# The compression's first layer as 128 adjoining columns, with the position embedding summed on GpSimd

## The chip, the cores and the metric

The kernel runs on one core of a Trainium2 chip. The metric is the device time of one execution in microseconds. The engines are named as in the profile: PE is TensorE (PEld its weight loads), DVE is VectorE, ACT is ScalarE, POOL is GpSimd, SP is SyncE, which issues most DMAs. SBUF is the on-chip memory, PSUM the accumulators that PE writes.

## The reference

A decoder trunk of two layers on one sequence of 256 tokens and 2048 features, all in float32. Layer 1 is HGRN2, a gated linear recurrence; layer 2 is native sparse attention with 16 heads in 4 groups. Each layer has one wide input projection, one output projection and a SiLU gate. What the change touches lies in layer 2: the compression of keys and values, and the softmax attention behind it.

```python
def compress_kv(kv, pe, w1, b1, w2):
    """kv (B,S,G,dk) -> compressed (B,G,n_cmp,dk): blocks of CMP_BLOCK with stride CMP_STRIDE, MLP phi."""
    chunks = kv.reshape(B, S // CMP_STRIDE, CMP_STRIDE, G, dk)
    blocks = jnp.concatenate([chunks[:, m:m + n_cmp] for m in range(ratio)], axis=2)
    blocks = blocks + pe[None, None, :, None, :].astype(blocks.dtype)
    flat = blocks.transpose(0, 3, 1, 2, 4).reshape(B, G, n_cmp, CMP_BLOCK * dk)
    return jax.nn.gelu(flat @ w1 + b1) @ w2
```

A block is 32 tokens, the stride is 16, so each block is two adjoining chunks of 16 positions and there are 15 blocks. `w1` has 32 x 128 rows and 128 columns. The embedding `pe` (32 positions of 128 features) adds the same vector `pe . w1` to the hidden layer of each block. This is done once for keys (K set) and once for values (V set).

## The kernel before

Nearly all the work is float32 matmuls at high precision: each operand is cut into a high part (`hi`, a cast to fp32r, by ACT) and a low part (`lo` = raw - hi, by DVE), and a product is three matmuls, hi.hi, hi.lo and lo.hi (`mm3`) or the like. The weights stream through SBUF in pieces of 128 x 1024 numbers, along a list `plan`. For each piece, SP loads it into one of six `raw` buffers (L126, L1095), ACT writes `hi` (L138), DVE writes `lo` (L148), and PE multiplies (L179 and L181 for the input projections, L156 elsewhere). `flush` walks the list in order: ahead of piece i's products it emits the casts up to piece i+3, the subtractions up to i+2 and the loads. There are four `hi` and four `lo` buffers. Each engine takes its instructions in the order in which the program emits them, and waits for semaphores.

Work that belongs to finished chunks (gathers, gates, attention) is written as generators; `advance` steps each of them once before and once after each piece's products, so one more `yield` moves what follows by half a piece.

The compression: `kc_done` collects the projected keys or values (`kz`, feature by token), `compress` splits them into `kh` and `kl`, and `w1_piece` puts four pieces of `w1` per set between the pieces of the next projection (K set: in the value projection's chunk `C_VC`, V set: in `C_KS`). Each piece has four positions of each half of a block. `compress_products` multiplies, for each of the 16 positions, 66 columns of `kh` and `kl` (64 chunks of the four groups, read with a stride of 16, and two columns that hold the embedding of both halves) by 256 columns of `w1` (both halves), three matmuls a position. `phi` then copies the 66 x 256 sums to SBUF, transposes them on PE (L830), adds both halves and the two embedding columns on DVE (L832 to L837), and goes on with GELU and the second layer.

The attention: for each of four groups, `attend` runs logits, softmax, transposes, `evacuate` (it splits the transposed weights into `ph`, `pl` and, for the compressed blocks, the corner tile `pc`) and `values`. `q_split` splits the queries of the next group, and `gated` applies SiLU to the gate `z` (with two loads of activation tables) and multiplies. The output tile of a group is `ot`.

## Time and profile before

| | |
|---|---|
| median of three runs | 986.13 us (985.73 to 987.29) |
| the profiled execution | 986.4 us, of it the span 984.6 us |
| granted TensorE clock | 0.998 |
| PE busy | 968.7 us, 6735 matmuls |
| DVE busy | 658.3 us, 1275 instructions |
| ACT busy | 569.5 us, 1056 instructions |
| POOL busy | 59.9 us, 154 instructions |
| first and last w1 product, K set | 534.3 to 548.5 us |
| transposes of `phi`, K set and V set | at 551.3 and 580.0 us |

A row of single instructions reads: start (us from the span's start), duration in us, engine, line, operation, what it writes and reads, shape, count, and in brackets the idle time of the engine ahead of it and what ended it. A row of a group reads: line, engine, operation, tiles, shape, count, then total busy us and mean ns of one, then the engine's idle time ahead of them and what ended most of it. A row of a stretch reads: from and to, length, then busy time and count of PE, PEld, DVE, ACT and POOL, the granted clock, the share of the DMA engines and GB/s. Matmuls are pipelined: the pace of PE is the distance from start to start, not the duration. Spans on POOL are rough.

### The profile page before, as it was taken

The numbers are of one execution on the slowest core, as the hardware profiler recorded it, in microseconds if no ns is written. First come the engines' busy times: TensorE is split into PE (matmuls) and PEld (weight loads), VectorE is DVE, ScalarE is ACT, GpSimd is POOL, SyncE is SP. The second block draws the span as 40 slices with busy tenths as digits, with TensorE's granted clock in tenths as the row PEclk, the third lists the DMA queues.
The fourth block names the chain that finished last, engine by engine and source line by source line (L and its number), as shares of the span: only waits on it lengthen the run. The fifth ranks groups of instructions, "written<-read, shape, count | busy, mean of one in ns | idle before, by whom it ended". The sixth has DMA issues, their size and how long they took to land.

```text
span 984.6 us, 17622 instructions
## 1 busy us (share of the span) xinstructions
PE 968.7 (98%) x6735; PEld 838.5 (85%) x6735; DVE 658.3 (67%) x1275; ACT 569.5 (58%) x1056; POOL 59.9 (6%) x154
## 2 busy tenths in 40 slices
PE   9999999999999999999999999999999999999996
PEld 8888888888888888888888888998888888888886
DVE  6796478646864786465566666567777778686654
ACT  6754565456545654554455555467677776875542
POOL 3101000100010001000020000000000000000000
PEclk9999999999999999999999999999999999999999
DMA  9655565556555655566777776565555545546662
GB/s 317 201 172 151 172 192 165 157 171 193 156 166 172 186 158 163 176 222 231 234 218 207 223 229 184 157 198 170 150 152 141 158 130 160 160 130 232 204 215 96
DMA packets 141524, 178.98 MB, mean 182 GB/s; under 512 B 6016, under 2 KB 102880, under 8 KB 141312
## 3 DMA queue, kind: packets, MB, share of 16 engines
q1 hardware_dynamic: 139424, 171.86, 56.8%
q0 software_dynamic: 1680, 5.46, 2.0%
q8 instruction: 53, 0.87, 0.4%
q10 hardware_dynamic: 336, 0.54, 0.1%
q14 instruction: 31, 0.25, 0.1%
HBM read 173.62 MB, written 4.22 MB: 181 GB/s over the span
## 4 chain that ended last, share of the span: by engine, by line
PE 80%; ACT 10%; DVE 6%; issue 2%; DMA 1%; SPq 0%; POOLq 0%; ACTq 0%; POOL 0%; DVEq 0%
PE mainps L156 40%; PE mainps L179 21%; PE mainps L181 11%; PE auxps L156 3%; ACT L L970 2%; ACT hi L138 2%; PE auxps L516 2%; DVE lo L148 1%; DVE L L963 1%; ACT ph L1004 1%; ACT L L979 1%; ACT pc L1006 1%; DMA xt<-in_x_dram 1%; DVE pc L1011 1%; ACT L1073 1%
## 5 line engine op out<-in xcount | busy, mean ns | idle before, releaser
L179 PE MATMUL mainps<-xx,hi 128*128 128x512 f32 x1280 | 454.9, 398 | 0.2 <-DVE Kg L313 0.2
L138 ACT CAST hi<-raw 128x1024 fp32r<-128x1024 f32 (+3 forms) x317 | 328.0, 1039 | 206.6 <-PE mainps L156 142.8
L148 DVE TENSOR_TENSOR lo<-raw,hi 128x1024 fp32r<-128x1024 f32 (+3 forms) x317 | 379.2, 1206 | 92.1 <-ACT hi L138 91.3
L181 PE MATMUL mainps<-xx,lo 128*128 128x256 f32 x1280 | 357.6, 279 | 0.1
L179 PEld LDWEIGHTS mainps<-xx,hi 128*128 128x128 f32 x1280 | 240.2, 188 | 54.6 <-DVE Kg L313 0.6
L181 PEld LDWEIGHTS mainps<-xx,lo 128*128 128x128 f32 x1280 | 241.4, 189 | 0.6 <-DVE lo L148 0.4
L156 PE MATMUL mainps<-hi,xx 128*128 128x512 f32 (+1 forms) x704 | 209.4, 375 | 0.0
L156 PEld LDWEIGHTS mainps<-hi,xx 128*128 128x128 f32 x704 | 128.4, 188 | 23.2
L156 PE MATMUL mainps<-lo,xx 128*128 128x512 f32 (+1 forms) x352 | 131.0, 372 | 0.0
L156 PE MATMUL mainps<-hi,yh 128*128 128x512 f32 (+1 forms) x288 | 106.0, 368 | 0.0
L156 PE MATMUL mainps<-hi,yl 128*128 128x512 f32 (+1 forms) x288 | 105.4, 366 | 0.0
L156 PE MATMUL mainps<-lo,yh 128*128 128x512 f32 (+1 forms) x288 | 105.3, 366 | 0.0
L156 PEld LDWEIGHTS mainps<-lo,xx 128*128 128x128 f32 x352 | 66.1, 188 | 10.4
L156 PEld LDWEIGHTS mainps<-hi,yl 128*128 128x128 f32 x288 | 54.3, 189 | 8.8
L156 PEld LDWEIGHTS mainps<-lo,yh 128*128 128x128 f32 x288 | 54.4, 189 | 8.5
L156 PEld LDWEIGHTS mainps<-hi,yh 128*128 128x128 f32 x288 | 54.4, 189 | 8.4
L970 ACT ACTIVATE L<-L,mx 128x128 f32<-128x128 f32 (+1 forms) x96 | 37.6, 393 | 31.0 <-DVE mx L965 31.0
L313 DVE TENSOR_TENSOR zs<-mainps,zs 128x256 f32<-128x256 f32 x48 | 19.0, 421 | 33.7 <-ACT zs L311 33.7
L567 POOL COPY ST<-S 32x128 f32<-32x128 f32 x32 | 21.6, 675 | 229.8 <-DVE S L524 228.8
L524 DVE COPY_PREDICATED S<-masks,auxps 128x128 f32<-128x128 uint32 x48 | 14.6, 303 | 28.8 <-PE auxps L557 15.9
L1008 DVE TENSOR_TENSOR pl<-auxps,ph 128x512 fp32r<-128x512 f32 (+1 forms) x32 | 17.7, 557 | 22.0 <-ACT ph L1004 20.4
L311 ACT COPY zs<-mainps 128x256 f32<-128x256 f32 x48 | 16.5, 373 | 13.5 <-PE mainps L181 13.2
(257 smaller groups left out, 905.2 us busy)
## 6 DMA issues: line engine op xcount, KB each, us to landing
raw<-in_hgrn_w_in_dram SPq DMA_DIRECT2D x127, 512.0 KB, 4.0
raw<-in_nsa_w_in_dram SPq DMA_DIRECT2D x104, 512.0 KB, 3.8
raw<-in_hgrn_w_out_dram SPq DMA_DIRECT2D x32, 512.0 KB, 4.7
raw<-in_nsa_w_out_dram SPq DMA_DIRECT2D x32, 512.0 KB, 4.0
raw<-in_nsa_w_in_dram SPq DMA_DIRECT2D x10, 420.0 KB, 3.9
xt<-in_x_dram SPq DMA_DIRECT2D x8, 256.0 KB, 7.9
raw<-in_x_dram SPq DMA_DIRECT2D x4, 512.0 KB, 4.2
x_dram<-x POOLq DMA_DIRECT2D x4, 512.0 KB, 6.0
```

The source lines that it names most:

```text
L138: nc.scalar.copy(hi[:, :m], raw[:, :m])
L148: nc.vector.tensor_sub(lo[:, :m], raw[:, :m], hi[:, :m].bitcast(F32))
L156: nc.tensor.matmul(dst, a, b, start=first and n == 0, stop=last and n == 2, skip_group_check=True)
L179: nc.tensor.matmul(ps, hv[:, fs], xx[:, k].rearrange("p a t -> p (a t)"), start=k == 0, stop=False, skip_group_check=True)
L181: nc.tensor.matmul(ps[:, S:], lv[:, fs], xh[:, k], start=False, stop=k == KT - 1, skip_group_check=True)
L311: nc.scalar.copy(o, p[:, S:])
L313: nc.vector.tensor_add(o, p[:, :S], o)
L516: nc.tensor.matmul(dst[32 * b:32 * b + 32, j] if cols == 32 else dst[32 * b:32 * b + 32, :, j], k[:, cs], qs, start=True, stop=True, tile_ ...
L524: nc.vector.copy_predicated(S32, masks[:, i, None, :].to_broadcast([P, 4, 32]), bank[:, n])
L567: nc.gpsimd.tensor_copy(ST[rs, :, 0:3:2, rs], S32[rs].rearrange("p (h t) c -> p h t c", h=2))
L970: nc.scalar.activation(dst, dst, AF.Exp, bias=mx[:, i:i + 1], accum_out=sm[:, i:i + 1])
L1008: nc.vector.tensor_sub(pl[:, ks, hh, :], t, ph[:, ks, hh, :].bitcast(F32))
```

## The change

1. `compress` writes one tile `kk` of 16 positions by 128 columns: for each position, 64 columns of high parts and behind them 64 of low parts. `compress_products` needs two matmuls a position, `w1`'s `hi` and `lo` against these 128 columns. The lo.lo product comes with it. The embedding's two columns are gone.
2. The embedding's share is computed on POOL: as soon as DVE has made `lo` of a w1 piece, `embedding` multiplies the raw piece in place by the embedding (a scalar per feature and position), folds 1024 columns in three additions to 128, and adds these to `pew`, a strip of the scratch tile. In `phi` one matmul with `pew` as stationary side and a column of ones sums over the features.
3. `phi` transposes 128 x 128 twice and adds four parts instead of two.
4. `kk` takes the place of `kh` and `kl`; the groups' output tiles share its buffer as one tile of two halves.
5. In the attention, `q_split` and `gated` get one more `yield` ahead, and `evacuate` handles the corner `pc` between the two pieces of `ph` and `pl`.

```diff
-    def add_own(load, fn, done=None):
-        plan.append((dict(load=load, fn=fn, done=done, before=None), None, bool(done)))
+    def add_own(load, fn, done=None, see=None):
+        plan.append((dict(load=load, fn=fn, done=done, before=None, see=see), None, bool(done)))
...
         nc.vector.tensor_sub(lo[:, :m], raw[:, :m], hi[:, :m].bitcast(F32))
         if kts is None:
+            ch["see"](raw)
             parts[i] = hi, lo
             return
...
-        NS["abs"] = scratch[:66, 256:512]
+        NS["abs"] = scratch[:, 256:512]
+        NS["pew"] = scratch[:, 644:772]
...
-    def compress(name, kz, pe0):
-        ns = NS["p2"]
-        kh = ns.tile([P, 66 * 16], F32R, tag="ot", name="kh")
-        kl = ns.tile([P, 66 * 16], F32R, tag="ot", name="kl")
-        pe = pcol[:, 1, pe0:pe0 + 32]
-        srcs = [(slice(512 * j, 512 * j + 512), kz[j].rearrange("p a t -> p (a t)")) for j in range(2)]
-        srcs.append((slice(1024, 1056), pe))
-        yield
-        for cs, src in srcs:
-            nc.scalar.copy(kh[:, cs], src)
-        yield
-        yield
-        for cs, src in srcs:
-            nc.vector.tensor_sub(kl[:, cs], src, kh[:, cs].bitcast(F32))
-        NS[name] = [t.rearrange("p (m q) -> p m q", q=16) for t in (kh, kl)]
+    def compress(name, kz):
+        kk = NS["kk"] = NS["p2"].tile([P, 16, P], F32R, tag="kk", name="kk", bufs=1)
+        by_position = lambda part, j: kk[:, :, 64 * part + 32 * j:64 * part + 32 * j + 32].rearrange("p q m -> p m q")
+        srcs = [(j, flat(kz[j]).rearrange("p (m q) -> p m q", q=16)) for j in range(2)]
+        yield
+        for j, src in srcs:
+            nc.scalar.copy(by_position(0, j), src)
+        yield
+        yield
+        for j, src in srcs:
+            nc.vector.tensor_sub(by_position(1, j), src, by_position(0, j).bitcast(F32))
...
-            kh, kl = NS[name]
-            wh, wl = (t.rearrange("p (a q c) -> p a q c", a=2, q=4) for t in (wh, wl))
+            kk = NS["kk"]
+            parts_ = [t.rearrange("p (a q c) -> p a q c", a=2, q=4) for t in (wh, wl)]
             for q in range(4):
-                mm3(NS[name, "ps"][:66, :256], kh[:, :, 4 * i + q], kl[:, :, 4 * i + q], wh[:, :, q, :], wl[:, :, q, :],
-                    i == 0 and q == 0, i == 3 and q == 3)
+                for n, w in enumerate(parts_):
+                    nc.tensor.matmul(NS[name, "ps"][:, :256], kk[:, 4 * i + q, :], w[:, :, q, :],
+                                     start=i == 0 and q == 0 and n == 0, stop=i == 3 and q == 3 and n == 1,
+                                     skip_group_check=True)
...
+    def embedding(pe0, i):
+        def see(raw):
+            w, acc = raw.rearrange("p (a q c) -> p a q c", a=2, q=4), NS["pew"]
+            pe = pcol[:, 1, pe0 + 4 * i:pe0 + 4 * i + 4]
+            pe = bass.AP(tensor=pe.tensor, offset=pe.offset, ap=[list(pe.ap[0]), [16, 2], [1, 4], [0, P]])
+            nc.gpsimd.tensor_tensor(w, w, pe, op=ALU.mult)
+            for n in (512, 256, 128):
+                nc.gpsimd.tensor_tensor(raw[:, :n], raw[:, :n], raw[:, n:2 * n], op=ALU.add)
+            if i == 0:
+                nc.gpsimd.tensor_copy(acc, raw[:, :P])
+            else:
+                nc.gpsimd.tensor_tensor(acc, acc, raw[:, :P], op=ALU.add)
+        return see
...
-            nc.tensor.transpose(abt[:, a * 66:(a + 1) * 66], abs_[:, a * P:(a + 1) * P], ident[:66, :66])
+            nc.tensor.transpose(abt[:, a * P:(a + 1) * P], abs_[:, a * P:(a + 1) * P], ident)
+        nc.tensor.matmul(abt[:, 256:257], NS["pew"], NS["one"], start=True, stop=True)
         yield
-        nc.vector.tensor_add(bia, b1, abt[:, 64:65])
-        nc.vector.tensor_add(bia, bia, abt[:, 66 + 65:66 + 66])
-        av = abt[:, 0:64].rearrange("p (g m) -> p g m", g=G)
-        bv = abt[:, 66:130].rearrange("p (g m) -> p g m", g=G)
+        nc.vector.tensor_add(bia, b1, abt[:, 256:257])
+        av, al, bv, bl = (abt[:, 64 * n:64 * n + 64].rearrange("p (g m) -> p g m", g=G) for n in range(4))
         nc.vector.tensor_scalar(hid, av[:, :, :NCMP], bia, None, op0=ALU.add)
+        nc.vector.tensor_add(hid, hid, al[:, :, :NCMP])
         nc.vector.tensor_add(hid, hid, bv[:, :, 1:])
+        nc.vector.tensor_add(hid, hid, bl[:, :, 1:])
...
     def q_split(g, a, q):
+
+        yield
...
-            for t, ks in srcs:
+
+            for n, (t, ks) in enumerate(srcs):
                 nc.scalar.copy(ph[:, ks, hh, :], t)
-            for tt in range(2):
-                nc.scalar.copy(pc[64:64 + NCMP, tt], t2[32 * tt:32 * tt + NCMP, 256:384])
-            for t, ks in srcs:
+                for tt in range(2 - 2 * n):
+                    nc.scalar.copy(pc[64:64 + NCMP, tt], t2[32 * tt:32 * tt + NCMP, 256:384])
+            for n, (t, ks) in enumerate(srcs):
                 nc.vector.tensor_sub(pl[:, ks, hh, :], t, ph[:, ks, hh, :].bitcast(F32))
...
-                    ot = ns.tile([P, 66 * 16], F32, tag="ot", name="ot")
...
+                    if g == 0:
+                        NS["ot"] = ns.tile([P, 2, 1024], F32, tag="kk", name="ot", bufs=1)
+                    ot = NS["ot"][:, g % 2]
...
     def gated(g, zs):
         ks = [slice(4 * g + 2 * a, 4 * g + 2 * a + 2) for a in range(2)]
+        yield
         for a in range(2):
             nc.scalar.activation(zs[a], zs[a], AF.Silu)
...
-        return lambda: add_own(load, compress_products(name, i), done if i == 3 else None)
+        return lambda: add_own(load, compress_products(name, i), done if i == 3 else None, embedding(pe0, i))
```

Three places of the order show what moves. First, POOL between the opening of layer 2 and the attention. Before (`Vc` and `pc` are cleared, `scratch` gets the second layer's weights, `bias` is the attention's bias):

```order
L771 MEMSET scratch 128x4
L775 MEMSET Vc 128x512
L775 MEMSET pc 128x512
L776 DMA scratch<-in_nsa_phi_k_w_dram 128x128
L777 DMA scratch<-in_nsa_phi_v_w_dram 128x128
L928 DMA bias<-bias_dram 128x2x256 x2
```

Now, up to the second w1 piece of the K set:

```order
L779 DMA scratch<-in_nsa_phi_v_w_dram 128x128
L829 TENSOR_TENSOR raw<-raw,pcol 128x1024
L831 TENSOR_TENSOR raw<-raw 128x512
L831 TENSOR_TENSOR raw<-raw 128x256
L831 TENSOR_TENSOR raw<-raw 128x128
L833 COPY scratch<-raw 128x128
L829 TENSOR_TENSOR raw<-raw,pcol 128x1024
```

Five operations for each of eight w1 pieces now stand between the weights' loads and the bias loads; `scratch` in them is the strip `pew`, and from the second piece of a set on the copy is an addition at L835.

Second, PE at the end of a set, where the transposes of `phi` lie in the stream of the next projection. Before:

```order
L179 MATMUL mainps<-xx,hi 128x512
L181 MATMUL mainps<-xx,lo 128x256
L830 MATMUL auxps<-ident,scratch 128x66 x2
L179 MATMUL mainps<-xx,hi 128x512
L181 MATMUL mainps<-xx,lo 128x256
```

Now:

```order
L180 MATMUL mainps<-xx,hi 128x512
L182 MATMUL mainps<-xx,lo 128x256
L846 MATMUL auxps<-ident,scratch 128x128 x2
L847 MATMUL auxps<-one,scratch 128x1
L180 MATMUL mainps<-xx,hi 128x512
L182 MATMUL mainps<-xx,lo 128x256
```

The matmul with `pew` (L847) is new, and stands at the same place as the transposes, ahead of the next piece's products.

Third, ACT where a gate's SiLU and an evacuation meet in the attention. Before:

```order
L311 COPY zs<-mainps 128x256 x2
L1073 ACT_TABLE_LOAD
L1073 ACTIVATE zs<-zs 128x512 x2
L1076 ACT_TABLE_LOAD
L1076 ACTIVATE one<-one 128x1
L138 CAST hi<-raw 128x1024
L1004 CAST ph<-auxps 128x4x128
L1004 CAST ph<-auxps 128x2x128
L1006 CAST pc<-auxps 15x128 x2
L138 CAST hi<-raw 128x1024
L1085 CAST yh<-zs 128x512
```

Now:

```order
L312 COPY zs<-mainps 128x256 x2
L138 CAST hi<-raw 128x1024
L1024 CAST ph<-auxps 128x4x128
L1026 CAST pc<-auxps 15x128 x2
L1024 CAST ph<-auxps 128x2x128
L1097 ACT_TABLE_LOAD
L1097 ACTIVATE zs<-zs 128x512 x2
L1100 ACT_TABLE_LOAD
L1100 ACTIVATE one<-one 128x1
L138 CAST hi<-raw 128x1024 x2
```

The SiLU with its two table loads went from ahead of the evacuation to behind it, and `pc` went between the two pieces of `ph`.

More of the change, by code (lines that the diff above doesn't have):

```diff
@@ L784, in zs_take, with kc_done @@
         return z
-    def kc_done(name, *args):
+    def kc_done(name):
         def done(a, ps):
@@ L825, in phi @@
         hid, t1 = hid_all[:, :, :NCMP], NS["gelu"][:, :, :NCMP]
-        nc.scalar.copy(abs_, ab[:66, :256])
+        nc.scalar.copy(abs_, ab[:, :256])
         yield
@@ L1002, in evacuate @@
             pc = NS["pc"][:, hh]
-            for t, ks in srcs:
+            for n, (t, ks) in enumerate(srcs):
                 nc.scalar.copy(ph[:, ks, hh, :], t)
-            for tt in range(2):
-                nc.scalar.copy(pc[64:64 + NCMP, tt], t2[32 * tt:32 * tt + NCMP, 256:384])
-            for t, ks in srcs:
+                for tt in range(2 - 2 * n):
+                    nc.scalar.copy(pc[64:64 + NCMP, tt], t2[32 * tt:32 * tt + NCMP, 256:384])
+            for n, (t, ks) in enumerate(srcs):
                 nc.vector.tensor_sub(pl[:, ks, hh, :], t, ph[:, ks, hh, :].bitcast(F32))
-            nc.vector.tensor_copy(pc[0:NCMP], pc[64:64 + NCMP].bitcast(F32))
-            for tt in range(2):
-                nc.vector.tensor_sub(pc[32:32 + NCMP, tt], t2[32 * tt:32 * tt + NCMP, 256:384],
-                                     pc[64:64 + NCMP, tt].bitcast(F32))
+                if n == 0:
+                    nc.vector.tensor_copy(pc[0:NCMP], pc[64:64 + NCMP].bitcast(F32))
+                for tt in range(2 - 2 * n):
+                    nc.vector.tensor_sub(pc[32:32 + NCMP, tt], t2[32 * tt:32 * tt + NCMP, 256:384],
+                                         pc[64:64 + NCMP, tt].bitcast(F32))
         def values(a, half):
@@ L1087, in gated, with w1_piece @@
             nc.vector.tensor_sub(yl[:, ks[a]], zs[a], yh[:, ks[a]].bitcast(F32))
-    def w1_piece(name, w1, i, b1, finish):
+    def w1_piece(name, w1, i, b1, pe0, finish):
         wv = w1[0].rearrange("(a q d) c -> d a q c", a=2, d=P)
```

14 lines of the change are left out of this document (7 added, 7 removed).

## The prediction

> **What bounds the kernel now.** I read the page first (engine shares), then the chain of waits over the compression's stretch, then the groups of TensorE instructions with the idle time ahead of them in the attention, and last single instructions on GpSimd and VectorE.
>
> ```profile
> span 984.6 us, 17622 instructions
> ...
> PE 968.7 (98%) x6735; PEld 838.5 (85%) x6735; DVE 658.3 (67%) x1275; ACT 569.5 (58%) x1056; POOL 59.9 (6%) x154
> ```
>
> TensorE (PE) is busy for 98% of the span. VectorE (DVE) is at 67%, GpSimd (POOL) at 6%. The busy time by stage, and the chain between 525 and 600 us, where the compression lies:
>
> ```profile
> 530.00:560.00 30.00, 30.00 (x190) 26.90 (x188) 20.58 (x30) 16.75 (x22) 0.00 (x0) 1.00 0.71 212
> ...
> 700.00:890.00 190.00, 184.10 (x1132) 163.02 (x1131) 144.87 (x404) 139.93 (x342) 5.51 (x18) 1.00 0.52 153
> ```
>
> ```profile
> by line: PE mainps L179 55.4%; PE mainps L181 27.8%; PE auxps L156 15.4%; PE auxps L875 1.3%; PE auxps L830 0.3%; PE auxps L869 0.2%
> ```
>
> In the compression PE never waits (30.00 of 30.00), so each matmul less is time less, and each wait that is put ahead of PE is time more. In the attention PE idles 5.9 of 190 us. POOL does nothing from 530 to 560 us.
>
> **The matmuls that go.** One w1 piece of the compression, its first and last row, and the rows ahead of it and behind it:
>
> ```profile
> 534.20 0.28 PE L181 MATMUL mainps<-xx,lo 128*128 128x256 f32 x1
> 534.32 0.28 PE L156 MATMUL auxps<-hi,kh 128*66 128x256 f32 x1
> ...
> 535.62 0.28 PE L156 MATMUL auxps<-hi,kl 128*66 128x256 f32 x1
> 535.74 0.40 PE L179 MATMUL mainps<-xx,hi 128*128 128x512 f32 x1
> ```
>
> Twelve matmuls take 535.74 - 534.32 = 1.42 us, 0.119 us each. Four of twelve go in each of 8 pieces: 32 x 0.119 = 3.8 us. The stationary side grows from 66 to 128 columns; the row ahead has 128 and streams 256 columns too, and the next matmul starts 0.12 us after it (534.20 to 534.32), so I add nothing for that. In each `phi`, the two transposes grow from 66 to 128 columns and one matmul by a single column is added; before, the two took 0.10 us (551.28 to 551.38 below). I put 0.2 us each, 0.4 together. Sum: -3.4 us.
>
> **The attention's order.** The groups with idle time ahead of them, 700 to 895 us:
>
> ```profile
> L156 PE MATMUL auxps<-Kh,qh 128*128 128x272 f32 (+1 forms) x36 | 10.6, 294 | 1.2 <-DVE pl L1008 1.2
> L156 PE MATMUL auxps<-ph,Vsh 128*128 128x256 f32 x19 | 5.8, 303 | 3.0 <-DVE pc L1011 2.7 <-ACT ph L1004 0.2
> L156 PE MATMUL auxps<-pl,Vsh 128*128 128x256 f32 x19 | 5.7, 298 | 0.9 <-DVE pl L1008 0.9
> L1029 PE MATMUL auxps<-pc,Vc 79*128 79x256 f32 x13 | 4.0, 305 | 1.4 <-ACT hi L138 1.4
> ```
>
> ScalarE (ACT) around the first slow place:
>
> ```profile
> 734.51 1.28 ACT L1073 ACT_TABLE_LOAD   x1
> ...
> 738.26 0.20 ACT L1076 ACTIVATE one<-one 128x1 f32<-128x1 f32 x1
> 739.31 0.85 ACT L1004 CAST ph<-auxps 128x512 fp32r<-128x512 f32 x2
> ```
>
> 1.2 + 3.0 + 0.9 + 1.4 = 6.5 us. Ahead of the evacuation at 739.31 stands the SiLU with its two table loads, from 734.51 to 738.46, about 4 us; the added `yield` in `gated` puts it behind. That frees the 2.7 and the 1.2. The corner `pc` now comes ahead of the second piece of `pl`, which serves the 1.4; `q_split`'s `yield` takes a copy away from ahead of the evacuation, which serves the 0.9. Behind the moved SiLU wait the next `hi` casts and `exps`; before, they stood behind SiLU and evacuation both, so they lose nothing. Bounds 0 (as much comes back elsewhere) and 6.5; I take 5.2, four fifths, since SiLU's 3.9 is the plain part: -5.2 us.
>
> **GpSimd's sum, and the new wait.** Per w1 piece POOL now makes five operations: 1024, 512, 256, 128 and 128 columns, 2048 in all, serially dependent. The last sum of a set is the stationary side of a matmul in `phi`. PE takes its instructions in order, so the whole weight stream behind that matmul waits for POOL. That wait is not in the trace; its ends are.
>
> ```profile
> masks.py:199 POOL TENSOR_SCALAR_AFFINE_SELECT ident<-ident 128x128 f32<-128x128 f32 x1 | 0.3, 291 | 0.1
> ...
> L78 POOL TENSOR_SCALAR rs<-oss 128x4 f32<-128x4 f32 x8 | 1.5, 192 | 113.8 <-ACT y L617 113.8
> ```
>
> ```profile
> 114.73 0.19 POOL L78 TENSOR_SCALAR rs<-oss 128x4 f32<-128x4 f32 x1 [25.62 <-ACT y L617]
> 115.00 1.05 POOL L79 TENSOR_TENSOR rs<-rs,mhalf 128x4 f32<-128x4 f32 x1
> ```
>
> *Price.* With one input, (291 - 192) / 124 = 0.80 ns a column. Fixed are 0.19 us for four columns, and 115.00 - 114.73 = 0.27 until the next, dependent operation starts. A two-input operation has three streams: 0.8 ns a column if all overlap, 1.6 if the reads take turns, 2.4 to 2.5 if all do. I take 2.0, between the last two: POOL and VectorE take turns at their operands (the next rows), so I don't expect two reads of POOL's own to overlap. A piece: 2048 x 2.0 = 4.10 + 5 x 0.27 = 5.45 us unopposed; the ends are 2.99 and 6.47.
>
> The Trainium skill (GPSIMD Engine Reference, Performance versus the Vector engine) gives 4497 ns for a two-input add over 2048 columns, so (4497 - 192) / 2048 = 2.1 ns each as an estimate; by it, the sum below would be about 1.2 us higher. No run here shows it.
>
> *Contention.* POOL's copies in the first layer beside VectorE:
>
> ```profile
> L567 POOL COPY ST<-S x32: 292/392/1271, 69.5 to 385.3; 32x128 f32<-32x128 f32 x32
> ```
>
> ```profile
> 85.57 1.22 DVE L148 TENSOR_TENSOR lo<-raw,hi 128x1024 fp32r<-128x1024 f32 x1
> 85.73 1.21 POOL L567 COPY ST<-S 32x128 f32<-32x128 f32 x1 [13.95 <-DVE S L524]
> 86.71 0.51 DVE L501 TENSOR_TENSOR QL<-QL,TT 128x256 f32<-128x256 f32 x1
> ```
>
> ```profile
> L501 DVE TENSOR_TENSOR QL<-QL,TT x32: 414/420/514, 54.5 to 389.5; 128x256 f32<-128x256 f32 x32
> ```
>
> The copy that takes 0.29 us at best started at 85.73, inside a `lo` subtraction, and ended at 86.94, 0.15 after it; the next DVE operation, with two inputs from SBUF too, took 0.51 instead of 0.42, as long as the copy's 128 columns last. So they take turns whole, and `lo` is such an operation.
>
> The Trainium skill (SBUF — State Buffer, SBUF: two separate sides) says so: GpSimd and a VectorE operation with two SBUF inputs take one port pair as an exclusive lock for the whole instruction. The rows above agree. If they shared instead, the tally's figure without turns would be nearer.
>
> *The tally.* The second w1 piece of the K set is the first of the three `lo` at 535.99, done by 537.2. The row, VectorE's `lo` from there to `phi`, and PE at `phi`:
>
> ```profile
> 535.99 3.49 DVE L148 TENSOR_TENSOR lo<-raw,hi 128x1024 fp32r<-128x1024 f32 x3
> ```
>
> ```profile
> L148 DVE TENSOR_TENSOR lo<-raw,hi 128x1024 fp32r<-128x1024 f32 x7 | 8.5, 1223 | 3.8 <-ACT hi L138 3.8
> ```
>
> ```profile
> 551.28 0.28 PE L830 MATMUL auxps<-ident,scratch 66*128 66x66 f32 x2
> 551.38 0.48 PE L179 MATMUL mainps<-xx,hi 128*128 128x512 f32 x1
> ```
>
> The same for the V set, whose second w1 piece is the `lo` at 564.89:
>
> ```profile
> 564.89 1.22 DVE L148 TENSOR_TENSOR lo<-raw,hi 128x1024 fp32r<-128x1024 f32 x1
> ```
>
> ```profile
> L148 DVE TENSOR_TENSOR lo<-raw,hi 128x1024 fp32r<-128x1024 f32 x7 | 8.3, 1222 | 3.2 <-ACT hi L138 3.2
> L862 DVE TENSOR_TENSOR Kl<-zs,Kh 128x512 fp32r<-128x512 f32 x1 | 0.7, 684 | 0.0
> ```
>
> ```profile
> 579.96 0.28 PE L830 MATMUL auxps<-ident,scratch 66*128 66x66 f32 x2
> ```
>
> K set: POOL has three pieces left at 537.2: 3 x 5.45 = 16.35. Until `phi` VectorE has seven more `lo`, at (3.49 - 1.22) / 2 = 1.13 us from start to start 7.9 us, of which 7 x 0.27 = 1.9 fit into POOL's own gaps. End: 537.2 + 16.35 + 7.9 - 1.9 = 559.6. PE would be at `phi` at 551.28 - 4 x 0.48 = 549.4 (four pieces, each four matmuls of 0.119 us shorter). Stall: 10.2 us. V set: the `lo` ends at 566.1, and POOL, whose first piece VectorE still held up, starts at 566.7 as I estimate; with seven `lo` and one `Kl` (8.5 - 2.2): 566.7 + 16.35 + 6.3 = 589.4, against 579.96 - 1.92 = 578.0. Stall: 11.4 us. Together **21.6 us**; with 0.80 ns 2.8 + 3.4 = 6.2, with 2.5 ns 13.3 + 14.4 = 27.7. Without turns at 2.0 ns: 4.2 + 4.4 = 8.6, and none at 0.80. DVE's own lateness is inside it: `phi`'s additions and two `lo` behind them on DVE wait for the same matmul, but PE then has two split pieces in hand. The raw buffers are now held until POOL is through, and SyncE's loads wait in order behind them; I set that to nothing beyond the stall, since the last is free when the stall ends and its next piece is six pieces on. Behind POOL's sums in its own queue stand only the bias loads of the attention, a whole stage later.
>
> *Restart.* At its start PE ran 128-column matmuls at half pace for 4 us:
>
> ```profile
> 1.05 2.93 PE L1193 MATMUL auxps<-zeros 128*128 128x128 f32 x12 [1.05 <-DVE zeros L321]
> 5.07 1.68 PE L1193 MATMUL auxps<-ident 128*128 128x128 f32 x12
> ```
>
> 0.21 us each, then 0.11: some 2 us lost. Idle times in the trace are under 1 us, so whether a 10 us stall brings this back is open: 0 to 4.0 for two; I take 3.5, since PE at the start is the nearest case.
>
> The Trainium skill (TensorE: Matmul & The Clock Gate, Part 1: The HAM clock gate) says that an idle window of some 3.4 us halves the clock again; no run here shows it.
>
> Strided writes of `kk` by ScalarE and VectorE (two each per set) replace three contiguous ones; they hide behind the three pieces by which the split runs ahead, and I set them to nothing; without that cover they would add their own time, about two microseconds a set.
>
> **Sum.** -3.4 - 5.2 + 21.6 + 3.5 = +16.5 us. The profiled execution took 986.4 us (span 984.6 and 1.8 around it); the median is 986.13. Predicted: 986.1 + 16.5 = 1002.6 us.
>
> **Rivals.** (1) *POOL is in time*, the side of faster: its three pieces end before 549.4 when each takes under (549.4 - 537.2) / 3 = 4.07 us, that is under 1.33 ns a column, with no turns taken. For it: VectorE is idle a third of the time and streams may overlap. Against it: the copy at 85.73. Time: 986.1 - 8.6 = 977.5. (2) *Turns cost nothing*, only POOL's own chain is late: +8.6 and up to 4 of restart: 986 to 990. Against it the same row. (3) *Streams overlap, turns are taken*: +6.2 without restart: 983.7. (4) *All streams take turns*: 27.7 + 4.0 - 8.6: 1009. (5) *The change doesn't do what it says*: 128 columns cost what is saved, or the attention's gaps reappear: 5 us more on the forecast, 1008.
>
> **Chances.** Forecast 0.53 (its own range 995 to 1008), (1) 0.12, (2) 0.14, (3) 0.06, (4) 0.11, (5) 0.04. A measurement tells this kernel from no change at about 0.2%, 2 us. Faster: (1), most of (3): 0.16. Same: half of (2), the rest of (3): 0.08. Slower 0.76. The range leaves out (1) and what lies past (4): 983 to 1012.
>
> **What would show it.** Right: PE idle by some 10 us ahead of L847 in each set, released by POOL's L835; L829 near 2 us alone and longer beside `lo`; some `lo` over 1.22 us. The attention's four idle groups nearly empty; eight matmuls of 0.119 us a piece. Wrong: POOL's last sum done before PE's transposes, or L829 near 1 us.

## The result and the profile after

The changed kernel takes 997.86 us (median of 4 runs, 997.23 to 999.93), the kernel before, run beside it, 986.11 us (985.73 to 987.29). The ratio is 1.0121, with a 95% interval of 1.0103 to 1.0138: slower by 11.75 us. The prediction said 1002.6.

From the page after, the span and the busy time of each engine:

```profile
span 996.1 us, 17622 instructions
...
PE 967.2 (97%) x6707; PEld 838.0 (84%) x6707; DVE 669.3 (67%) x1275; ACT 569.9 (57%) x1054; POOL 114.6 (12%) x194
```

TensorE has 28 matmuls fewer and 1.5 us less of busy time, but the span is 11.5 us longer. POOL has 54.7 us more. The stretches of the K set, of the V set and of the attention, after:

```profile
530.00:560.00 30.00, 20.41 (x124) 17.69 (x123) 19.09 (x18) 13.62 (x17) 27.51 (x20) 0.91 0.36 111
570.00:600.00 30.00, 20.39 (x124) 17.53 (x123) 19.44 (x20) 12.98 (x19) 25.26 (x21) 0.93 0.41 127
720.00:910.00 190.00, 190.00 (x1183) 170.44 (x1183) 150.78 (x425) 144.91 (x351) 5.59 (x18) 1.00 0.54 163
```

In each set PE now stands idle for 9.6 of 30 us, while POOL is busy for over 25; in the attention, where it had idled 5.9 of 190 us, it never waits. What PE waited for, in the whole span (line, releaser, total, times, longest):

```profile
PE auxps L847 <- POOL scratch L835: 14.2, 2, 7.7
PE auxps L846 <- ACT scratch L842: 2.6, 2, 2.2
PE mainps L182 <- DVE lo L148: 2.5, 2, 1.6
```

L847 is the matmul with `pew`, L835 POOL's sum of a piece (the last of a set releases L847), L846 the transposes ahead of it in `phi`, L842 ACT's copy of the sums for these. 14.2 + 2.6 + 2.5 = 19.3 us, all of it in the two sets. ACT ahead of the wait at L846 in the K set:

```profile
550.56 1.04 ACT L138 CAST hi<-raw 128x1024 fp32r<-128x1024 f32 x1 [4.86 <-DMA raw<-in_nsa_w_in_dram]
551.51 0.37 ACT L842 COPY scratch<-auxps 128x256 f32<-128x256 f32 x1
```

The copy stands behind a `hi` that waited 4.86 us for its load, so this wait comes from a load. It costs nothing of its own: PE stands at L847 right behind it until 558.80 anyway. Single matmuls after, around the wait of each set:

```profile
551.93 0.44 PE L846 MATMUL auxps<-ident,scratch 128*128 128x128 f32 x2 [2.25 <-ACT scratch L842]
558.80 0.59 PE L847 MATMUL auxps<-one,scratch 128*128 128x1 f32 x2 [6.43 <-POOL scratch L835]
...
560.04 0.63 PE L180 MATMUL mainps<-xx,hi 128*128 128x512 f32 x1
...
560.68 0.63 PE L180 MATMUL mainps<-xx,hi 128*128 128x512 f32 x1
...
565.13 0.40 PE L180 MATMUL mainps<-xx,hi 128*128 128x512 f32 x1
...
565.48 0.39 PE L180 MATMUL mainps<-xx,hi 128*128 128x512 f32 x1
...
598.90 0.59 PE L847 MATMUL auxps<-one,scratch 128*128 128x1 f32 x2 [7.72 <-POOL scratch L835]
599.35 0.77 PE L180 MATMUL mainps<-xx,hi 128*128 128x512 f32 x1
...
602.67 0.40 PE L180 MATMUL mainps<-xx,hi 128*128 128x512 f32 x1
```

Read the starts. Behind the wait a pair of L180 and L182 (from one L180 to the next) takes 560.68 - 560.04 = 0.64 us, later 565.48 - 565.13 = 0.35: for 5.9 us (559.25 to 565.13) in the K set and 3.3 us (599.35 to 602.67) in the V set PE runs at half clock (granted clock 0.50). Nine pairs and five pairs lie there; at 0.348 us they would have taken 3.1 and 1.7 us, so this costs some 2.7 + 1.6 = 4.3 us.

POOL after, from the second w1 piece of each set to its last sum:

```profile
536.89 2.85 POOL L829 TENSOR_TENSOR raw<-raw,pcol 128x1024 f32<-128x1024 f32 x1
...
545.13 1.32 POOL L835 TENSOR_TENSOR scratch<-scratch,raw 128x128 f32<-128x128 f32 x1
...
553.33 1.89 POOL L829 TENSOR_TENSOR raw<-raw,pcol 128x1024 f32<-128x1024 f32 x1
555.30 2.92 POOL L831 TENSOR_TENSOR raw<-raw 128x512 f32<-128x512 f32 x3
558.30 0.45 POOL L835 TENSOR_TENSOR scratch<-scratch,raw 128x128 f32<-128x128 f32 x1
...
576.60 2.22 POOL L829 TENSOR_TENSOR raw<-raw,pcol 128x1024 f32<-128x1024 f32 x1 [3.58 <-DVE lo L148]
...
598.39 0.45 POOL L835 TENSOR_TENSOR scratch<-scratch,raw 128x128 f32<-128x128 f32 x1
```

No row behind the first of each set has idle time ahead of it: the three pieces are one unbroken chain of 21.9 us (536.89 to 558.75) and 22.2 us (576.60 to 598.84). The same operation takes 0.45 us at 558.30 and 1.32 at 545.13, where it starts inside the first of two `lo`:

```profile
544.66 2.88 DVE L148 TENSOR_TENSOR lo<-raw,hi 128x1024 fp32r<-128x1024 f32 x2
```

That `lo` ends at about 546.1 (two take 2.88 us), the sum at 546.45: it waits for the rest of one `lo` and then runs.

### The profile page after: what moved, and what is told of

Same layout as the page of the kernel before. It is cut to its first block, busy times and chain, and to the rows that moved or that the text cites. A ratio compares the mean times of both kernels' runs of the same rounds, so it can differ in the third digit from the quotient of the medians.

```text
span 996.1 us, 17622 instructions
## 1 busy us (share of the span) xinstructions
PE 967.2 (97%) x6707; PEld 838.0 (84%) x6707; DVE 669.3 (67%) x1275; ACT 569.9 (57%) x1054; POOL 114.6 (12%) x194
## 4 chain that ended last, share of the span: by engine, by line
PE 91%; POOL 5%; DVE 1%; issue 1%; DMA 1%; ACT 0%; SPq 0%; POOLq 0%; DVEq 0%; ACTq 0%
PE mainps L157 40%; PE mainps L180 28%; PE mainps L182 14%; PE auxps L157 3%; POOL raw L831 3%; POOL raw L829 2%; PE auxps L517 2%; PE auxps L1009 1%; DVE lo L148 1%; DMA xt<-in_x_dram 1%; PE auxps L583 0%; POOL scratch L835 0%; PE auxps L610 0%; PE auxps L611 0%; PE auxps L592 0%
## 5 line engine op out<-in xcount | busy, mean ns | idle before, releaser
L180 PE MATMUL mainps<-xx,hi 128*128 128x512 f32 x1280 | 458.9, 401 | 0.2 <-DVE Kg L314 0.2
L148 DVE TENSOR_TENSOR lo<-raw,hi 128x1024 fp32r<-128x1024 f32 (+3 forms) x317 | 388.9, 1238 | 94.5 <-ACT hi L138 94.0
L182 PE MATMUL mainps<-xx,lo 128*128 128x256 f32 x1280 | 359.6, 281 | 2.5 <-DVE lo L148 2.5
L180 PEld LDWEIGHTS mainps<-xx,hi 128*128 128x128 f32 x1280 | 242.3, 189 | 55.1 <-DVE Kg L314 0.6
L182 PEld LDWEIGHTS mainps<-xx,lo 128*128 128x128 f32 x1280 | 243.4, 190 | 3.9 <-DVE lo L148 3.7
L568 POOL COPY ST<-S 32x128 f32<-32x128 f32 x32 | 21.6, 674 | 229.2 <-DVE S L525 228.2
L831 POOL TENSOR_TENSOR raw<-raw 128x512 f32<-128x512 f32 (+2 forms) x24 | 28.2, 1174 | 1.9
```

Of the source, the lines that this page charges most:

```text
L148: nc.vector.tensor_sub(lo[:, :m], raw[:, :m], hi[:, :m].bitcast(F32))
L180: nc.tensor.matmul(ps, hv[:, fs], xx[:, k].rearrange("p a t -> p (a t)"), start=k == 0, stop=False, skip_group_check=True)
L182: nc.tensor.matmul(ps[:, S:], lv[:, fs], xh[:, k], start=False, stop=k == KT - 1, skip_group_check=True)
L568: nc.gpsimd.tensor_copy(ST[rs, :, 0:3:2, rs], S32[rs].rearrange("p (h t) c -> p h t c", h=2))
L831: nc.gpsimd.tensor_tensor(raw[:, :n], raw[:, :n], raw[:, n:2 * n], op=ALU.add)
```

## The experiments

All but `order_alone` start from the changed kernel. `no_sum` and `short_sum` leave out the embedding's share or most of it. Where each kernel ended, its ratio to the kernel before, and PE's listed waits in the profiled execution:

| run | what it is | us | ratio (95%) | PE waits in the compression |
|---|---|---|---|---|
| changed kernel | | 997.86 | 1.0121 (1.0103 to 1.0138) | 19.3 |
| order_alone | before + the attention's order | 976.09 | 0.9898 (0.9884 to 0.9913) | none |
| no_sum | without POOL's sum (share left out) | 973.17 | 0.9870 (0.9853 to 0.9886) | none |
| late | `phi` 14 yields later | 996.54 | 1.0101 (1.0086 to 1.0116) | 14.7 |
| fill | 48 transposes inside the wait | 996.22 | 1.0099 (1.0084 to 1.0114) | 6.8 |
| private | product in a tile of its own | 987.77 | 1.0012 (1.0003 to 1.0021) | 8.1 |
| late_tail | `phi` and its tail later | 993.03 | 1.0064 (1.0051 to 1.0077) | 10.7 |
| late_free | late_tail + private | 983.12 | 0.9975 (0.9959 to 0.9992) | 5.2 |
| short_sum | no folds (seven eighths of the share left out) | 975.85 | 0.9895 (0.9881 to 0.9909) | 1.5 |
| private_behind | private, but behind `lo` | 1000.82 | 1.0148 (1.0133 to 1.0164) | 21.5 |
| vector_sum | the sum on VectorE | 985.21 | 0.9992 (0.9983 to 1.0001) | 7.9 |
| early_sum | the sum in the first layer's output projection | 974.22 | 0.9878 (0.9861 to 0.9894) | none |

### The attention's order alone (order_alone)

```diff
     def q_split(g, a, q):
+        yield
...
-            for t, ks in srcs:
+            for n, (t, ks) in enumerate(srcs):
                 nc.scalar.copy(ph[:, ks, hh, :], t)
-            for tt in range(2):
-                nc.scalar.copy(pc[64:64 + NCMP, tt], t2[32 * tt:32 * tt + NCMP, 256:384])
+                for tt in range(2 - 2 * n):
+                    nc.scalar.copy(pc[64:64 + NCMP, tt], t2[32 * tt:32 * tt + NCMP, 256:384])
...
         ks = [slice(4 * g + 2 * a, 4 * g + 2 * a + 2) for a in range(2)]
+        yield
```

> The kernel before with the attention's new order alone: the two added yields and the evacuation in two pieces with pc between; compression untouched, no sum on GpSimd. From the two traces, TensorE's rows of the same name in the attention stand 21.2 us later after than before at its start and 11.2 us later at its end, so the order itself brings about 9.7 to 10 us, more than the 6.5 us that the four groups list as idle time. Theory: 986.1 - 9.7 = 976.4 us, with those groups' idle time at zero. Rival 1 (the listed idle time is all there was to win): 986.1 - 6.5 = 979.6. Rival 2 (the attention gained in the changed kernel because TensorE came to it 20 us later, with loads and splits further ahead): under 3 us, 983 or more.

It took 976.09 us, 10.2 less than before. The attention's 190 us are full:

```profile
700.00:890.00 190.00, 190.00 (x1182) 170.33 (x1181) 150.72 (x413) 145.68 (x352) 5.36 (x18) 1.00 0.56 161
```

That is 3.7 us more than the 6.5 us that the groups of before list as idle, so rivals 1 and 2 fall. Where the rest was is seen in single matmuls of before:

```profile
740.02 0.29 PE L156 MATMUL auxps<-Kh,ql 128*128 128x272 f32 x1
740.66 0.39 PE L156 MATMUL auxps<-Kh,qh 128*128 128x256 f32 x1 [0.35 <-DVE pl L1008]
740.89 0.28 PE L156 MATMUL auxps<-Kl,qh 128*128 128x256 f32 x1
```

and of the same place with the new order:

```profile
739.11 0.29 PE L156 MATMUL auxps<-Kh,ql 128*128 128x272 f32 x1
739.24 0.28 PE L156 MATMUL auxps<-Kh,qh 128*128 128x256 f32 x1
739.35 0.28 PE L156 MATMUL auxps<-Kl,qh 128*128 128x256 f32 x1
```

The idle time is counted from the end of the matmul before, 0.29 us behind its start, but the next one could have started 0.13 us behind it. Before: 740.02 to 740.89 is 0.87 us for two starts; now 739.11 to 739.35 is 0.24. This wait is listed with 0.35 us and cost 0.63: 0.16 is the overlap of two matmuls that is lost, 0.11 the slower start (0.23 us to the next one instead of 0.12). Before lists 14 such waits in the attention. If each cost as much on top, as an estimate from this one, 14 x 0.27 = 3.8 us on top of 6.5 gives 10.3, against 10.2 measured.

### Without the sum (no_sum)

```diff
         NS["pew"] = scratch[:, 644:772]
+        nc.gpsimd.memset(NS["pew"], 0.0)
...
         def see(raw):
-            w, acc = raw.rearrange("p (a q c) -> p a q c", a=2, q=4), NS["pew"]
-            ...
+            pass
```

> The changed kernel without GpSimd's five operations a piece; the column that they fill is zeroed once, so the embedding's share of the first layer is left out. All else stays: 128 adjoining columns, strided writes of kk, larger transposes, the added matmul, the order of the attention. Theory: eight pieces end 0.5 us sooner each (-4.1) and the attention gives its 9.7: 972.3 us, with no idle time ahead of the added matmul and full clock behind it; the changed kernel's whole loss (25.5 us against this) is GpSimd's sum. Rival: the strided writes, or the columns, cost time themselves: 976 or more. Second rival: part of the loss is not the sum's, with idle time left at the added matmul.

It took 973.17 us, and PE does not wait:

```profile
530.00:560.00 30.00, 30.00 (x186) 26.73 (x185) 22.25 (x31) 18.87 (x25) 0.00 (x0) 1.00 0.76 226
570.00:600.00 30.00, 30.00 (x179) 26.06 (x178) 19.43 (x30) 15.30 (x22) 0.11 (x1) 1.00 0.77 235
```

So POOL's sum costs the changed kernel 997.86 - 973.17 = 24.7 us, more than its whole loss, and the 128 columns bring 976.09 - 973.17 = 2.9 us by the medians of two runs beside each other. The strided writes cost nothing that is seen; neither rival holds.

### The matmul that waits, put later (late)

```diff
-        NS["pew"] = scratch[:, 644:772]
+        NS["pew"] = [scratch[:, 644:772], NS["p2"].tile([P, P], F32, tag="pew", name="pew", bufs=1)]
...
         nc.scalar.copy(abs_, ab[:, :256])
-        yield
+        for _ in range(14):
+            yield
```

> The changed kernel with the whole computation, in which phi pauses 14 yields (seven pieces) between its copy of the bank and its transposes, and the V set has a column tile of its own; so TensorE comes to the matmul that waits for GpSimd some 20 us later, and GpSimd's operations, their turns with VectorE and the raw buffers that they hold stay as they are. Theory (the loss is TensorE waiting in order behind one matmul, and the half clock behind that wait): 973 to 976 us, up to 4 above the kernel without the sum for the late lo; no idle time over 1 us ahead of the added matmul, full clock throughout. Rival (the turns that GpSimd takes from VectorE starve TensorE of split weights wherever the matmul stands): 985 or more, with the idle time moved to the weight stream.

It took 996.54 us: my theory fell. PE no longer waits at the matmul with `pew`; it waits in three other places. PE's waits in `late`, and those of SyncE's queue from 530 to 590 us:

```profile
PE auxps L887 <- DVE scratch L864: 6.1, 1, 6.1
PE mainps L182 <- DVE lo L148: 4.2, 4, 2.4
PE auxps L818 <- ACT hi L138: 3.7, 1, 3.7
```

```profile
SPq L126 <- POOL scratch L835: 14.1, 2, 8.1
SPq L1120 <- POOL scratch L835: 8.6, 1, 8.6
```

The 6.1 us are `phi`'s own tail: PE comes to its last matmul (L887) a fixed number of yields later, and VectorE, whose `lo` take turns with POOL, isn't there yet. The 3.7 us are a load: SyncE issues nothing between 553.95 and 563.03, because the next raw buffers are still POOL's. The rival had the place of the waits only in part (`lo`, 4.2 us), but its time was right. The two waits of 6.1 and 3.7 us were followed by half clock as well.

### PE kept busy inside the wait (fill)

```diff
             nc.tensor.transpose(abt[:, a * P:(a + 1) * P], abs_[:, a * P:(a + 1) * P], ident)
+        for _ in range(48):
+            nc.tensor.transpose(abt[:, 260:260 + P], ident, ident)
```

> The changed kernel with 48 transposes of the identity put ahead of the added matmul in each phi, written to unused columns of the same bank; some 5 us of work for TensorE inside the wait of 6.4 and 7.7 us. Theory (the half clock behind the wait is brought on by TensorE's idle time, and costs 2.5 + 1.6 = 4 us): 994 us, with 0.35 us for a pair of matmuls behind the wait in place of 0.64. Rival (the clock falls for another reason, or the transposes outlast the wait): 997.9 or more.

It took 996.22 us, 1.6 less than the change and not 4 (the profiled execution, the shortest of four, took 994.72). The K set, with the granted clock as the third number from the end:

```profile
553.00:556.00 3.00, 3.00 (x16) 3.00 (x16) 2.83 (x4) 1.34 (x3) 3.00 (x2) 0.50 0.17 26
556.00:559.00 3.00, 3.00 (x29) 3.00 (x29) 0.68 (x1) 1.01 (x2) 2.77 (x4) 0.99 0.44 149
559.00:562.00 3.00, 3.00 (x23) 2.79 (x22) 1.58 (x8) 2.98 (x4) 0.62 (x2) 1.00 0.32 95
```

Behind the fill the clock is full (1.00 from 559 us on, against 0.50 to 565 in the change), so the half clock does follow from PE's idle time. In the V set the fill took 5.4 us, PE waited 1.7 us more, and the clock was 1.00 throughout, against 0.50 from 599 to 602 in the change. But in the K set the 2.2 us of idle time ahead of the transposes had already brought the half clock on: the fill ran its first 3 us at 0.50 and took 6.8 us where I had counted 5, so PE came to L849 0.2 us behind POOL's last sum. In the V set a wait of 2.0 us for `lo`, ending at 578.5, brought 0.50 from 580 to 583 us. The theory holds for the cause; the 4 us that it names (4.3 by the starts above) were not to be won this way.

### The product in a tile of its own (private), and the same behind `lo` (private_behind)

```diff
-            nc.gpsimd.tensor_tensor(w, w, pe, op=ALU.mult)
+            prod = NS["p2"].tile([P, 6, 2, P], F32, tag="ph", name="prod", bufs=1).rearrange("p a b c -> p (a b c)")[:, :PIECE]
+            nc.gpsimd.tensor_tensor(prod.rearrange("p (a q c) -> p a q c", a=2, q=4), w, pe, op=ALU.mult)
             for n in (512, 256, 128):
-                nc.gpsimd.tensor_tensor(raw[:, :n], raw[:, :n], raw[:, n:2 * n], op=ALU.add)
+                nc.gpsimd.tensor_tensor(prod[:, :n], prod[:, :n], prod[:, n:2 * n], op=ALU.add)
```

> The changed kernel with GpSimd's product written to a tile of its own, where the three folds go on; so a w1 piece's raw buffer is read by GpSimd for one operation and not for four, and the loads behind it are not held. In the changed kernel GpSimd's operations follow each other without a pause to the last sum, so their end sets the wait, whatever the loads do. Theory: 996 to 998 us as changed; the idle time of 2.25 us ahead of the transposes (L846) goes, that ahead of the added matmul grows by as much. Rival (late loads are part of the loss): 994 or less.

It took 987.77 us, ten less than the change, against my theory. The rival's number came true; whether for its reason was open, since the tile changes two things. POOL in `private`:

```profile
519.25 2.35 POOL L830 TENSOR_TENSOR prod<-raw,pcol 128x1024 f32<-128x1024 f32 x1 [6.24 <-DMA raw<-in_nsa_phi_k_w_dram]
```

and the first piece in the changed kernel:

```profile
529.80 2.81 POOL L829 TENSOR_TENSOR raw<-raw,pcol 128x1024 f32<-128x1024 f32 x1 [17.43 <-DVE lo L148]
```

Writing in place, POOL must let `hi` and `lo` read the piece first; with a tile of its own it only needs the load, and starts 10.5 us sooner (519.25 against 529.80). The other thing is that the raw buffer is free sooner. The kernel that keeps the tile and gives the early start back:

```diff
+            nc.gpsimd.tensor_copy(prod[:, 0:1], lo[:, 0:1].bitcast(F32))
             nc.gpsimd.tensor_tensor(prod.rearrange("p (a q c) -> p a q c", a=2, q=4), w, pe, op=ALU.mult)
```

> The run with GpSimd's product in a tile of its own was 10 us faster than the change, against what I expected of it. Its trace shows two things that the tile changes: the product no longer writes the raw piece, so it needn't wait for hi and lo to have read it, and GpSimd starts the second K piece at 525.1 us instead of 536.9; and the raw buffer is free after one of five operations, so the loads behind it are issued up to 9 us sooner. This kernel keeps the tile and takes the first away: ahead of each product GpSimd copies one column of lo into the tile (written over by the product), so it starts behind lo as in the change. Theory A (the late start is what matters, the raw buffers are not): 994 to 998 us, with stalls of 7 to 10 us at the added matmul again. Theory B (the raw buffers' loads are what matters): 987 to 989, as with the tile alone.

It took 1000.82 us, with the whole wait back at the matmul with `pew`, L849 here, released by POOL's last sum:

```profile
PE auxps L849 <- POOL scratch L837: 20.6, 2, 10.9
```

The time is past theory A's 998 and far from B's: with the start back behind `lo`, the whole wait is back. But the kernel gives back more than the start. The product, which frees the raw buffer, now comes late too, and SyncE issues the first w1 load of the V set at 557.49 us, as in the change (558.78) and not as in `private` (547.80); so this run alone does not part the start from the loads. For the start speaks POOL's chain in the K set: from the second piece to the last sum it has no idle time for a load to cause, in the change, here and in `private`. There it runs from 525.12 to 553.63 us, longer than in the change (28.5 us against 21.9, with 12 `lo` in its way instead of 7), and still ends 5.1 us sooner since it starts 11.8 us sooner. A run with late starts and early loads was not made. Of the 3 us above the change, the listed waits show 2.2: the copy of one column (0.18 to 1.12 us) is one operation more a piece, and the K set's chain takes 22.8 us and starts 1.3 us later.

### Phi's tail and the loads taken out as well (late_tail, late_free)

```diff
         nc.scalar.copy(abs_, ab[:, :256])
-        yield
+        for _ in range(12):
+            yield
...
+        for _ in range(3):
+            yield
         nc.vector.tensor_add(bia, b1, abt[:, 256:257])
...
-        yield
-        yield
+        for _ in range(4):
+            yield
         nc.vector.tensor_mul(hid, hid, t1)
-        yield
+        for _ in range(5):
+            yield
```

> The run that paused phi by 14 yields, with 12 instead, and more yields behind the added matmul (3, 2, 4 and 5 where 1, 2, 2 and 1 stood), so that no later step of phi is reached by an engine before its operands are there; raw buffers held as in the changed kernel. In the trace of the run with 14, TensorE waited 6.1 us ahead of phi's last matmul for VectorE, 3.7 and 3.4 us for hi and lo of late loads, which SyncE issued only at 563.0 when GpSimd ended its last operation, and ran at half clock behind both. Theory (two covers had to be kept: phi's tail and the loads): the 6.1 and the half clock behind it (about 3) go, the late loads stay: 986 to 989 us. Rival (the turns themselves starve TensorE): no gain over the 14 yields, 994 or more.

> The kernel of the longer tail, and GpSimd's product in a tile of its own as well: the raw buffer is free behind the first of the five operations. Theory: with neither the added matmul, nor the tail, nor the loads waiting for GpSimd's chain, what is left is the late lo (0.9 us in the K set, 1.6 to 2 in the V set by the traces): 974 to 978 us, against 973.2 without the sum; SyncE's loads without a pause of 9 us. Rival (turns starve TensorE): 985 or more, with the waits on lo.

They took 993.03 and 983.12 us, against 986 to 989 and 974 to 978: both theories promised too much. The waits that I named went (no L887; with the tile no `hi` either), and the tile was worth 9.9 us. But more stayed than I had allowed. What is left in `late_free`, and its `lo` from 515 to 600 us:

```profile
PE auxps L818 <- DVE lo L148: 3.1, 2, 1.9
PE mainps L182 <- DVE lo L148: 2.1, 2, 1.2
```

```profile
L148 DVE TENSOR_TENSOR lo<-raw,hi 128x1024 fp32r<-128x1024 f32 x34 | 55.4, 1671 | 1.0 <-ACT hi L138 1.0
```

`lo` takes 1.67 us in the mean instead of 1.22, and VectorE has 1.0 us of idle time ahead of it in 85 us: it has become late for PE, 5.2 us in four waits, the last two of them followed by half clock (0.50 from 571 to 577.7 us, about 3 us). So the turns, by the late `lo`, do cost TensorE time here, some 10 us against `no_sum` with the half clock; the rival of `late` was right in this much.

### A shorter sum (short_sum)

```diff
             nc.gpsimd.tensor_tensor(w, w, pe, op=ALU.mult)
-            for n in (512, 256, 128):
-                nc.gpsimd.tensor_tensor(raw[:, :n], raw[:, :n], raw[:, n:2 * n], op=ALU.add)
```

> The changed kernel without the three folds: GpSimd multiplies a piece and adds its first 128 columns to the sum, so seven eighths of the embedding's share are left out. Two operations of 1.89 and 0.45 us a piece, which take a turn with one lo each: at most 2.4 + 2 x 1.1 = 4.6 us in place of 7.3. Theory (the stall is the chain's length against what TensorE needs for the three pieces): K set's chain ends at 537 + 3 x 4.6 = 551 at the latest and TensorE comes to the matmul at about 549: stalls of 0 to 2 us a set and no half clock: 973 to 977 us. Rival (the stall is not proportional to the chain, since each product of 1024 columns holds lo up whatever follows): 985 or more.

It took 975.85 us, as the theory said: one wait, for `lo`, of 1.5 us in the V set, and full clock. So nothing is wrong with a sum on POOL that PE waits for in order, as long as its chain ends before PE comes to it.

### The sum on VectorE (vector_sum)

```diff
+            for n in range(8):
+                col = pcol[:, 1, pe0 + 4 * i + 16 * (n // 4) + n % 4:][:, :1]
+                w = raw[:, n * P:(n + 1) * P]
+                if i == 0 and n == 0:
+                    nc.vector.tensor_scalar(acc, w, col, None, op0=ALU.mult)
+                else:
+                    nc.vector.scalar_tensor_tensor(acc, w, col, acc, op0=ALU.mult, op1=ALU.add)
```

> The changed kernel with the same sum computed by VectorE, straight behind lo: eight operations a piece, each column block times its embedding column plus the sum so far, 128 columns each; raw is only read and GpSimd does nothing. At 1.19 ns a column (lo's 1.22 us for 1024) and some 0.07 us besides, about 0.22 us each, 1.8 us a piece, 14 us in all, in a stretch of 65 us where VectorE is busy some 42; GpSimd's sum takes 41 us of the port by the unopposed durations. Theory (the loss comes from the sum being on GpSimd: its turns, and the length of its chain): 973 to 976 us, under 2 us of idle time for lo, none ahead of the added matmul. Rival (the stretch has no room for the sum on VectorE either): 980 or more, lo late by over 4 us in all.

It took 985.21 us, no better than before: the rival. VectorE from 515 to 600 us:

```profile
L148 DVE TENSOR_TENSOR lo<-raw,hi 128x1024 fp32r<-128x1024 f32 x31 | 36.9, 1219 | 1.0 <-ACT hi L138 1.0
L833 DVE SCALAR_TENSOR_TENSOR scratch<-raw,pcol,scratch 128x128 f32<-128x128 f32 x62 | 21.8, 352 | 2.0
```

One of the eight operations takes 0.35 us, not 0.22; 62 of the 64 are 21.8 us, where I had allowed 14 for all. `lo` is untouched (1.22 us, no turns), but late: PE waits for it five times, 7.9 us. In these two forms the sum has no room in this stretch on either engine; a cheaper form on VectorE was not tried.

### The sum where there is room (early_sum)

```diff
+    def early_sums(pool):
+        accs = [pool.tile([P, P], F32, name=f"pew{n}") for n in range(2)]
+        for n, (w1, b1) in enumerate(((phi_k_w1, 49), (phi_v_w1, 50))):
+            wv = w1[0].rearrange("(a q d) c -> d a q c", a=2, d=P)
+            for i in range(4):
+                raw = pool.tile([P, PIECE], F32, name=f"early{n}{i}")
+                w, acc = raw.rearrange("p (a q c) -> p a q c", a=2, q=4), accs[n]
+                for a in range(2):
+                    nc.sync.dma_start(w[:, a], wv[:, a, 4 * i:4 * i + 4])
...
+                for _ in range(5):
+                    yield
+        for _ in range(14):
+            yield
+        bp = aux_bank()
+        for n in range(2):
+            nc.tensor.matmul(bp[:, n:n + 1], accs[n], mhalf[:, :1], start=True, stop=True)
+        yield
+        for n in range(2):
+            nc.vector.scalar_tensor_tensor(bcol[:, n:n + 1], bp[:, n:n + 1], -2.0, pcol[:, 0, 49 + n:50 + n],
+                                           op0=ALU.mult, op1=ALU.add)
```

> The changed kernel with the same sum by the same five operations on GpSimd, moved out of the compression: the eight w1 pieces are loaded a second time, into buffers of their own, two and a half pieces apart during the output projection of the first layer, where every piece keeps TensorE for 2.8 us; two matmuls by a single column and two additions then make the bias of both sets ahead of the second layer, and phi adds it from there. Same instructions, same turns with VectorE, but nothing in order behind them: no raw buffer, no matmul of phi, and no piece of 1 us among those whose lo they hold up. Theory (GpSimd's operations are harmless where each lo that takes turns with them has a piece of 2.8 us to hide in, 1.1 + 1.9 us at the worst): 973 to 976 us, with lo at up to 3 us there and TensorE's idle time below 1 us in all. Rival (each turn costs TensorE time wherever it falls, or the eight loads more do): 980 or more.

It took 974.22 us, 1.2% less than before and the fastest kernel here that computes everything (`order_alone`'s interval overlaps with its). A stretch of the output projection, with POOL's busy time as the fifth one:

```profile
450.00:475.00 25.00, 25.00 (x116) 20.79 (x115) 19.86 (x16) 12.29 (x17) 23.96 (x18) 1.00 0.90 297
```

and `lo` from 420 to 520 us there, then the same row of the kernel before:

```profile
L148 DVE TENSOR_TENSOR lo<-raw,hi 128x1024 fp32r<-128x1024 f32 x36 | 60.6, 1712 | 7.7 <-ACT hi L138 7.6
```

```profile
L148 DVE TENSOR_TENSOR lo<-raw,hi 128x1024 fp32r<-128x1024 f32 x36 | 43.5, 1223 | 21.8 <-ACT hi L138 21.7
```

POOL is busy for 24 of 25 us, `lo` is as slow as in `late_free` (1.71 us), and PE never waits. The difference that I see is what PE asks for: 36 `lo` in 100 us here, one every 2.8 us; in the compression of before, seven from 537.2 to 551.28, one every 2.0. VectorE still has 7.7 us of idle time ahead of `lo`, of 21.8 before. That this pace alone decides was not varied by itself: the raw buffers are free here too, and nothing of `phi` waits.

## Why the prediction was right, and where it was off

The sign and the cause held; the time was 4.7 us too high, nearly all of it by one term.

**The w1 matmuls, -3.4.** 2.9 by the medians. Right within what two runs can tell.

**The attention's order, -5.2.** Measured alone: -10.2. This is the step that failed. The mechanism was right, SiLU, `pc` and the queries' split out of the way, but the size was bounded by "0 and 6.5", the listed idle time, and four fifths of it taken. All of it went, and by the one wait taken apart above each of the 14 cost some 0.27 us more than its listed time. The upper bound should have been worked out from starts, as the prediction's own row for one w1 piece was.

**GpSimd's sum, +21.6, and the restart, +3.5.** Together 25.1; measured 24.7. The chains were to end 22.4 us (537.2 to 559.6) and 22.7 us (566.7 to 589.4) behind their start; they took 21.9 and 22.2. The stalls were to be 10.2 and 11.4; the waits in each set are 0.90 + 2.25 + 6.43 = 9.6 and 1.56 + 0.33 + 7.72 = 9.6 us, most of them at L847. So the stall was taken 1.8 us too high in the V set and 0.6 in the K set, and the restart too low: 4.3 against 3.5, just past its range of 0 to 4.0. That their sum came so near is partly luck. Some 1.2 us of the 24.7 are in no listed wait, as in the attention. The restart was taken from PE's half pace at the start, but the trace shows a granted clock of 1.00 there (1 to 5 us), so it is not shown to be the same thing; what the runs show is 0.50 behind the waits.

**The price.** 2.0 ns a column and 0.27 us for each operation. Late in the V set POOL's rows are nearly unopposed:

```profile
L831 POOL TENSOR_TENSOR raw<-raw 128x512 f32<-128x512 f32 x1 | 1.3, 1261 | 0.1
...
L831 POOL TENSOR_TENSOR raw<-raw 128x128 f32<-128x128 f32 x1 | 0.5, 454 | 0.1
```

An addition costs (1261 - 454) / 384 = 2.10 ns a column; the multiplication less, 1893 ns at best for 1024, about 1.7. The five together are 1.89 + 1.26 + 0.72 + 0.45 + 0.45 = 4.8 us and five pauses of some 0.08, 5.2 us, against 5.45. So the value taken between 0.80 and 2.5 was near the true one; 2.10 is 2.6 times the 0.80 of one input, as if the streams of one operation hardly overlapped. The Trainium skill (GPSIMD Engine Reference, Performance versus the Vector engine) has a time for an addition from which the prediction estimated 2.1; the trace agrees.

**The turns.** As forecast: 1.89 to 2.88 us for the product, 0.45 to 1.32 for the last sum, `lo` up to 2.9. Without them three pieces would have taken 15.6 us and not 21.9. The Trainium skill (SBUF — State Buffer, SBUF: two separate sides) calls it an exclusive lock for a whole instruction; the rows agree.

**"Raw buffers: nothing beyond the stall".** True of the change, whose chain has no idle time between its second piece and its end, but only because the stall was there. With PE's wait moved away (`late`), SyncE's queue stood still for 9 us behind POOL and PE waited for the load instead. The step was right, and misleading about what a cure would bring. What the prediction didn't name at all is that the chain starts late because it writes in place; the count from the end of `lo` was right for that reason.

**The rivals.** (1), POOL in time at under 4.07 us a piece: that side exists and `short_sum` stands on it, but 5.2 us is past it before any turn. (2) and (3) fall with the turns and the 2.10 ns. (4) asked for 2.4 to 2.5 ns a column, which the 2.10 doesn't reach; its time of 1009 was 11 us too high. (5): the columns and the order both did what they say.

**The signs.** Idle time ahead of L847 of 6.4 and 7.7 us instead of some 10, released by L835; L829 at 1.89 us at best and 2.9 beside `lo`; the attention without idle groups: all there, the first smaller than told.

## What to carry to other kernels

A sum on an idle engine isn't free where its result is a matmul's operand: count its chain from the moment its input is free (an in-place write waits for every other reader) to the instruction that waits for it, with a turn for each of its operations that meets a two-input VectorE operation. Moving the waiting instruction only uncovers what it hid: the loads, the tail, the neighbour's lateness. Move the work to a stretch whose pieces leave the neighbour time, and when pricing TensorE's small waits, measure from start to start, not by the listed idle time.
